# A hybrid recurrent and attention decoder trunk on one core: half of the first head pair's key transfers issued from ScalarE's queue

## The chip, the core and the metric

The kernel runs on one core of one Trainium2 chip. The metric is the device time of one execution in microseconds, the median over runs; lower is better. A core has five engines that work side by side, each through its own list of instructions in order: TensorE (PE, matrix products into the accumulator memory, PSUM), VectorE (DVE), ScalarE (ACT), GpSimd (POOL) and SyncE (SP, which here only issues transfers). They wait for each other through semaphores. Transfers (DMAs) are issued by an engine's queue and carried out by the core's 16 DMA engines.

## What is computed

A trunk of two layers over 1024 positions of width 1024: layer 0 mixes positions with a gated linear recurrence, layer 1 with stick-breaking attention of 16 heads of 64, and each is followed by a SwiGLU network of width 2816. The part around the change is the attention:

```
def stick_breaking_attention(x, w_qkv, w_o):
    qkv = jnp.einsum("bsd,de->bse", x, w_qkv).reshape(bsz, seq, 3, N_HEADS, HEAD_DIM)
    ...
    for blk in range(seq // Q_BLOCK):
        ...
        z = jnp.einsum("bhqd,bhkd->bhqk", qb, kb).astype(jnp.float32) * scale
        strict = s_idx < t_idx
        log_fail = jnp.where(strict, jax.nn.log_sigmoid(-z), 0.0)
        suffix = lax.cumsum(log_fail, axis=3, reverse=True) - log_fail
        weights = jnp.where(strict, jnp.exp(jax.nn.log_sigmoid(z) + suffix), 0.0)
        outs.append(jnp.einsum("bhqk,bhkd->bhqd", weights.astype(vb.dtype), vb))
    ...
    return jnp.einsum("bse,ed->bsd", o, w_o)
```

All of it is in float32. The kernel splits a float32 factor into a high part (a cast to a shorter format that PE multiplies fast) and a low part (the rest), and makes a product from three matmuls: high by high, high by low, low by high.

## The kernel before

**Stages.** The program goes through the recurrent layer, the first SwiGLU network, the attention, and the second SwiGLU network with the output projection. The first projection of the attention starts on PE at 941 us, the last at 1394 us.

**The attention's tiling.** Heads go in eight pairs q = 0 to 7; a pair fills the 128 partitions, head 0 of the pair (hx = 0) in the lower 64 and head 1 in the upper 64. For each pair there are three projections (`which` = 0 query, 1 key, 2 value), each in two halves of 512 positions (n = 0, 1), each in eight steps over the model width (tile `qk_ps`, lines 655 to 657, three matmuls a step). VectorE scales a finished half into `t` (line 2047), ScalarE casts it into the high part `qh` (line 2051), and VectorE subtracts to get the low part `ql` (line 2055). The names are the same for queries and keys.

**The transfers that the change is about.** Scores multiply over 128 partitions, in which a head's high and low query parts lie one above the other (tile `q`), while the head's key part is there twice: `kh` holds the high part in both halves of the partitions, `kl` the low part in both. So each half of a key (q, n) needs eight transfers of 64 partitions by 512 elements, from SBUF to SBUF: for head hx and y = 0 to 3, x = 4 hx + y; y // 2 picks `kh` or `kl`, and y % 2 the half of the partitions that is written. A query's half needs four. They are issued in `move`, line 2070, all from SyncE's queue. In the first pair there are 8 query and 16 key transfers.

**From scores to output.** A chunk of scores `z_ps` (line 2108) is two matmuls, `kh` by `q` and `kl` by `q`, for one block of 128 queries and 128 to 512 keys; two PSUM banks alternate, so a chunk is held back until ScalarE has taken the one before last. ScalarE's sigmoid turns it into `F` (line 2120), VectorE scans that along the keys (lines 2127, 2129), PE transposes the result into `wt_ps` (line 2139), ScalarE and VectorE split it into `th` and `tl`, and PE multiplies with the values (`av_ps`, line 2156). The first four chunks of a head take the first half of its keys, the fifth (query block 4, keys 3 and 4, 256 columns) spans both halves.

**What sets the order.** The order of instructions is made by a planner (`Plan`, lines 37 to 77), which knows each task's engine, an assumed duration, what it depends on and a rank. It starts, again and again, the task that can begin first, and by rank among equals; the order of starting is the order in every engine's list. The engine "dma" stands for SyncE's queue: an issue holds it 0.55 us and lands after the task's 2.4 us. `attention_plan` gives it the whole attention. The projections, of which the next pair's always wait to be done, are spread between the score chunks by their ranks. A task on an engine name that no other uses is a mere delay.

**Completion counters.** In the built program each transfer that SyncE or ScalarE issues counts up one of eight semaphores (DMAHW0 to DMAHW7), given out in turn in the order in which the planner issued them. Before a transfer is issued, its queue waits until the earlier one on the same counter has landed.

Of the kernel before, what the change touches and what calls it, by code (L numbers as in the profile page):

```python
# [245 lines left out]
def key_span(q, hx, j, ci):  # L246
    kbs = [kb for kb in range(j + 1) if key_spot(q, hx, j, kb)[0] == ci]
    return kbs[0] * P, len(kbs) * P


def attention_plan(plan, fn, at):
    NP, LEAD = HEADS // 2, 8
    diag = lambda h, js: [(*h, j, j // 4) for j in js]
# [19 lines left out]
    act = lambda n: 0.08 + n * 0.00082  # L273
# [4 lines left out]
    def weights(i, name, r, raw, use):  # L278
        ld = known.get(name) or plan.add("dma", 4.8, fn["load", name], [raw], r - 4)
        h0 = plan.add("act", 0.5, fn["whi", name, 0], [ld, use], r - 2.5)  # L280
        l0 = plan.add("dve", 0.6, fn["wlo", name, 0], [h0], r - 2.3)
        h1 = plan.add("act", 0.5, fn["whi", name, 1], [h0], r - 2.1)
        wlo[name] = (l0, plan.add("dve", 0.6, fn["wlo", name, 1], [h1, l0], r - 1.9))
        wraw[i] = wlo[name][1]
# [7 lines left out]
    for n in range(NH):  # L292
        t = plan.add("act", 0.5, fn["s_hi", n], [known["acc", n]], -17 + 2 * n)
        t = plan.add("dve", 1.2, fn["s_lo", n], [t], -17 + 2 * n)
        t = plan.add("pe", 0.46, fn["sums", n], [t], -17 + 2 * n)
        t = plan.add("act", 0.62, fn["root", n], [t], -17 + 2 * n, "root")
        t = plan.add("act", 0.5, fn["square", n], [t], -17 + 2 * n)
        t = plan.add("dve", 0.66, fn["newton", n], [t], -17 + 2 * n)
        factors.append(plan.add("dve", 0.66, fn["rbc", n], [t], -17 + 2 * n))
    for i, (q, which, n) in enumerate(groups):  # L300
        s, wi = 24 * (q - 1) + 4 * (i % 6), 3 * q + which
        if n == 0 and wi:
            weights(wi, (q, which), s, wraw.get(wi - 3), wuse.get(wi - 2))
        p = None
        for k in KS:
            need = [p]
            if p is None:
                need.append(pt.get(i - 4 if i in (4, 5) else i - 2) if i > 3 else None)
            if q == 0:
                need += [known.get(("x", k, n))]  # L310
            need.append(wlo[q, which][k // 4] if wi else known[q, which])
            p = plan.add("pe", 0.705, fn["proj", q, which, n, k], need, s + len(need) / 100 + KS.index(k) / 2 + 0.5)
        proj[i] = wuse[wi] = p
        s += 4
        turned_by = factors[n] if q == 0 else None
        if which < 2:
            order.append(i)
            was = order[-3] if len(order) > 2 else None
            pt[i] = plan.add("dve", 0.6, fn["t", q, which, n], [p, turned_by, *moves.get(was, ())], s + 0.1)
            th = plan.add("act", 0.5, fn["qh", q, which, n], [pt[i], *moves.get(was, ())], s + 0.2)  # L320
            tl = plan.add("dve", 0.6, fn["ql", q, which, n], [th], s + 0.3)
            old = [(zlast, q - 2)] if q > 1 else []
            for x in range(4 + 4 * which):
                src = (tl if x % 2 else th) if which == 0 else (tl if x // 2 % 2 else th)
                m = plan.add("dma", 2.4, fn["move", q, which, n, x], [src, *old], s + 0.3 + x / 100)
                moved.setdefault((q, which, n, x // (2 + 2 * which)), []).append(m)
                moves.setdefault(i, []).append(m)
        else:
            old = [(vadd, (q - 2, x)) for x in range(2)] if q > 1 else []
            pt[i] = plan.add("dve", 0.6, fn["t", q, which, n], [p, turned_by, *old], s + 0.1)  # L330
            before = (dv, (q, n - 1) if n else (q - 1, 1)) if q or n else None
            turned = (turn, (q, n - 1) if n else (q - 1, 1)) if q or n else None
            dv[q, n] = plan.add("dve", 0.66, fn["dv", q, n], [pt[i], before, turned], s + 0.4)
            if q == NP - 1:
                for y in range(NP - 1 - n):
                    back[y, n] = [
                        plan.add("dma", 2.4, fn["back", y, n, x], [p, (kept, (y, n))], s + 0.5 + y / 10) for x in range(2)
                    ]
# [3 lines left out]
    for c, (q, hx, j, ci) in enumerate(chunks):  # L342
        s, dg = c - LEAD, j // 4 == ci
        k0, n = key_span(q, hx, j, ci)
# [26 lines left out]
    for u, (q, hx, G, kb) in enumerate(units):  # L371
        if u in turns:
            v = turns[u]
            old = [(avlast, v[0] - 2)] if v[0] > 1 else []
# [5 lines left out]
        n = len(js) * P  # L380
# [10 lines left out]
        s = u + 1  # L391
# [15 lines left out]
    s, out = 24 * (NP - 1), []  # L407
# [112 lines left out]
def trunk(  # L520
# [15 lines left out]
    nc = tc.nc  # L536
    out_t = out[0 : D * LATE].rearrange("(d p c) -> d p c", p=P, c=LATE)
    out_r = out[D * LATE : D * S].rearrange("(r c) -> r c", c=D)
    f32 = lambda t: t.bitcast(F32)
# [321 lines left out]
    with ExitStack() as st:  # L861
# [153 lines left out]
        with tc.manual_schedule(engines={E.PE, E.Activation, E.DVE, E.Pool}):  # L1015
            plan = Plan(pe=28.5, dve=39.3, act=36.0, dma=20.0)
# [969 lines left out]
    with ExitStack() as st:  # L1986
# [15 lines left out]
        pair = lambda tag, q: [own([P, S], f"{tag}{2 * (q % 2) + hx}", F32R, tag) for hx in range(2)]  # L2002
        raws, W, PS, TT, TH, TL = {}, {}, {}, {}, {}, {}
        Q, KH, KL, VT, DV, VV, F_, Z = {}, {}, {}, {}, {}, {}, {}, {}
# [50 lines left out]
            V.tensor_sub(TL[n], TT[n], f32(TH[n]))  # L2055

        def move(q, which, n, x):
            if n == x == 0:
                if which == 0:
                    Q[q] = pair("q", q)  # L2060
                else:
                    KH[q], KL[q] = pair("kh", q), pair("kl", q)
            cs = slice(n * NB, (n + 1) * NB)
            hx, y = divmod(x, 2 + 2 * which)
            src = sides[hx]
            if which == 0:
                dst, t, to = Q[q][hx], (TH, TL)[y][n], sides[hx ^ y]
            else:
                dst, t, to = (KH, KL)[y // 2][q][hx], (TH, TL)[y // 2][n], sides[y % 2]
            nc.sync.dma_start(f32(dst)[to, cs], f32(t)[src])  # L2070

        def v_diff(q, n):
            DV[q, n] = own([P, NB], "dv")
# [112 lines left out]
        def ob_part(o, k):  # L2186
# [11 lines left out]
            "qh": q_hi,  # L2198
            "ql": q_lo,
            "move": move,  # L2200
            "dv": v_diff,
            "vt": v_turn,
# [41 lines left out]
        with tc.manual_schedule(engines={E.PE, E.Activation, E.DVE, E.Pool, E.SP}):  # L2244
            plan = Plan(pe=0.0, **pre["free"])
            chunks, units = attention_plan(plan, Steps(acts), pre["at"])
            plan.emit()
            mix.load(2)
# [60 lines left out]
```

## Time and profile before

| | before |
|---|---|
| runs | 2150.68, 2151.21, 2151.43 us |
| median | 2151.21 us |
| the profiled execution | 2151.21 us |
| its span, first to last instruction | 2149.4 us |
| mean granted clock of TensorE | 0.999 |
| busy in the span: PE | 2140.9 us |
| busy in the span: DVE, ACT | 1710.3 us, 1090.9 us |
| HBM read and written | 176.88 MB, 70.78 MB |

The span runs from the first instruction to the last; the execution's own time has 1.81 us more around it. Times in rows of a timeline are counted from the span's start. A row reads: start, duration, engine, source line, operation, output and inputs, and in brackets how long the engine was idle before it and what ended that. "SPq" and "ACTq" are issues of transfers by SyncE and ScalarE, which don't count as busy; "x2" means two in a row, whose duration is then that of both.

### The profile page before, as it was taken

The page shows a single profiled execution, that of the slowest core. Times are in us where ns is not written, and L with a number is a line of the kernel's source. Part 1 is how long each engine was busy: PE and PEld are TensorE (multiplying, and loading weights), DVE is VectorE, ACT ScalarE, POOL GpSimd, SP SyncE. Part 2 cuts the span into 40 slices and gives each one's busy share as a digit, 9 for nine tenths or more (in the row PEclk, how much of TensorE's full clock was granted, in tenths as well). Part 3 has the DMA queues.
Part 4 walks back from the last instruction along what each step waited for, and adds up shares of the span by engine and source line. Part 5 has one row for each costly group of instructions (what it writes and reads, how often), then busy time and mean ns, then how long its engine had stood idle before and what let it go on. Part 6 is the DMA issues. An engine that isn't in the chain of part 4 may idle for free.

```text
span 2149.4 us, 27088 instructions
## 1 busy us (share of the span) xinstructions
PE 2140.9 (100%) x9952; PEld 1784.5 (83%) x9952; DVE 1710.3 (80%) x2417; ACT 1090.9 (51%) x1795; POOL 29.3 (1%) x41
## 2 busy tenths in 40 slices
PE   9999999999999999999999999999999999999998
PEld 8888888888888888888888888888888888888887
DVE  8978679667777887888888888878877777788887
ACT  6677445344434544665555555544633444454555
POOL 0000020000000000000000000002000000000000
PEclk9999999999999999999999999999999999999999
DMA  4111312344454764444333333542234444467442
GB/s 178 40 49 50 128 40 88 99 137 147 133 162 133 274 203 126 147 143 104 98 98 96 101 99 97 175 148 80 73 104 128 152 134 150 146 233 240 137 155 86
DMA packets 133316, 274.61 MB, mean 128 GB/s; under 512 B 15296, under 2 KB 23872, under 8 KB 133184
## 3 DMA queue, kind: packets, MB, share of 16 engines
q1 hardware_dynamic: 132768, 272.36, 40.0%
q8 instruction: 78, 1.28, 0.2%
q10 hardware_dynamic: 416, 0.52, 0.1%
q14 instruction: 54, 0.44, 0.1%
HBM read 176.88 MB, written 70.78 MB: 115 GB/s over the span
## 4 chain that ended last, share of the span: by engine, by line
PE 99%; DVE 0%; DMA 0%; ACT 0%; issue 0%; SPq 0%; DVEq 0%
PE p_ps L1218 39%; PE p_ps L1222 19%; PE qk_ps L655 4%; PE qk_ps L657 4%; PE qk_ps L656 4%; PE av_ps L2156 3%; PE z_ps L2108 3%; PE wt_ps L2139 3%; PE ob_ps L657 2%; PE a_ps L655 2%; PE a_ps L656 2%; PE ob_ps L655 2%; PE a_ps L657 2%; PE ob_ps L656 2%; PE a_ps L809 1%; PE g_ps L656 1%
## 5 line engine op out<-in xcount | busy, mean ns | idle before, releaser
L1218 PE MATMUL p_ps<-vh,wch 128*128 128x512 f32 x524 | 203.9, 389 | 0.0
L1218 PE MATMUL p_ps<-vh,wbh 128*128 128x512 f32 x524 | 203.9, 389 | 0.0
L1218 PE MATMUL p_ps<-vl,wbh 128*128 128x512 f32 x524 | 203.9, 389 | 0.0
L1218 PE MATMUL p_ps<-vl,wch 128*128 128x512 f32 x524 | 203.9, 389 | 0.0
L1218 PE MATMUL p_ps<-vl,wah 128*128 128x512 f32 x524 | 203.8, 389 | 0.0
L1218 PE MATMUL p_ps<-vh,wah 128*128 128x512 f32 x524 | 203.8, 389 | 0.0
L1167 ACT CAST wbh<-sb 128x1024 fp32r<-128x1024 f32 (+2 forms) x69 | 69.6, 1009 | 188.6 <-DVE sb L1151 188.6
L2120 ACT ACTIVATE F<-z_ps 128x512 f32<-128x512 f32 (+3 forms) x188 | 88.6, 490 | 119.7 <-PE z_ps L2108 117.7
L1222 PE MATMUL p_ps<-vh,wbl 128*128 128x512 f32 x524 | 142.1, 389 | 0.0
L1222 PE MATMUL p_ps<-vh,wcl 128*128 128x512 f32 x524 | 141.8, 389 | 0.0
L1222 PE MATMUL p_ps<-vh,wal 128*128 128x512 f32 x524 | 141.8, 389 | 0.0
L2127 DVE TENSOR_TENSOR_SCAN F<-F,unit 128x256 f32<-128x256 f32 (+3 forms) x128 | 105.5, 845 | 38.4 <-ACT F L2120 38.1
L2144 ACT CAST th<-wt_ps 128x512 fp32r<-128x512 f32 x192 | 92.2, 480 | 64.3 <-PE wt_ps L2139 39.4
L1218 PEld LDWEIGHTS p_ps<-vh,wch 128*128 128x128 f32 x524 | 98.3, 188 | 20.6
L1218 PEld LDWEIGHTS p_ps<-vh,wbh 128*128 128x128 f32 x524 | 98.3, 188 | 20.6
L1222 PEld LDWEIGHTS p_ps<-vh,wcl 128*128 128x128 f32 x524 | 98.3, 188 | 20.5
L1222 PEld LDWEIGHTS p_ps<-vh,wbl 128*128 128x128 f32 x524 | 98.3, 188 | 20.5
L1222 PEld LDWEIGHTS p_ps<-vh,wal 128*128 128x128 f32 x524 | 98.3, 188 | 20.4
L1218 PEld LDWEIGHTS p_ps<-vh,wah 128*128 128x128 f32 x524 | 98.3, 188 | 20.4
L1218 PEld LDWEIGHTS p_ps<-vl,wah 128*128 128x128 f32 x524 | 98.3, 188 | 20.4
L1218 PEld LDWEIGHTS p_ps<-vl,wbh 128*128 128x128 f32 x524 | 98.4, 188 | 20.4
L1218 PEld LDWEIGHTS p_ps<-vl,wch 128*128 128x128 f32 x524 | 98.3, 188 | 20.4
(447 smaller groups left out, 5416.8 us busy)
## 6 DMA issues: line engine op xcount, KB each, us to landing
raw<-in_ffn_w_in SPq DMA_DIRECT2D x88, 512.0 KB, 3.7
vl<-pd SPq DMA_DIRECT2D x128, 256.0 KB, 3.6
pd<-U SPq DMA_DIRECT2D x90, 256.0 KB, 2.3
raw<-in_ffn_w_out SPq DMA_DIRECT2D x28, 512.0 KB, 4.0
raw<-in_attn_w_qkv SPq DMA_DIRECT2D x24, 512.0 KB, 3.6
kh<-qh SPq DMA_DIRECT2D x64, 128.0 KB, 2.3
kl<-ql SPq DMA_DIRECT2D x64, 128.0 KB, 2.3
acc<-pd SPq DMA_DIRECT2D x28, 256.0 KB, 2.6
```

The source lines that it names most:

```text
L655: nc.tensor.matmul(ps, lhsT=wh, rhs=mh, start=first, stop=False, **kw)
L656: nc.tensor.matmul(ps, lhsT=wh, rhs=ml, start=False, stop=False, **kw)
L657: nc.tensor.matmul(ps, lhsT=wl, rhs=mh, start=False, stop=last, **kw)
L1167: nc.scalar.copy(self.full(self.wb), self.full(self.sb))
L1218: nc.tensor.matmul(ps, lhsT=c(hi, j), rhs=t, start=j == x == 0 and not onto, stop=False, skip_group_check=onto)
L1222: nc.tensor.matmul(ps, lhsT=c(lo, j), rhs=rhs[j][0], start=False, stop=j == len(rhs) - 1, skip_group_check=onto)
L2108: nc.tensor.matmul(ps[:, 0:n], lhsT=lhsT, rhs=rhs, start=i == 0, stop=i == 1)
L2120: nc.scalar.activation(F, Z.pop(c)[:, 0:n], AF.Sigmoid, scale=-SC)
L2127: V.tensor_tensor_scan(rev, rev, unit[:, NB - n :][:, ::-1], 0.0, op0=ALU.mult, op1=ALU.add)
L2139: nc.tensor.transpose(tp[:, c : c + P], F_[q, hx, j, ci][:, k0 : k0 + P], ident)
L2144: nc.scalar.copy(WH[u][:, c:], TP[u][:, c:])
L2156: nc.tensor.matmul(ps[:, c:], lhsT=VV[q][:, kb, hx], rhs=t.pop(u)[:, c:], start=kb == 4 * G and i == 0, stop=kb == 3 and i == 1,)
```

## The change

Of the first head pair's key transfers (q = 0, which = 1), those with odd x, the ones that write the upper 64 partitions, are issued from ScalarE's queue; the other 8 key transfers, and all transfers of queries and of the other pairs, stay on SyncE's. For the planner such a transfer is a task of 0.6 us on ScalarE, ranked right behind the high cast, and a delay of 1.85 us till it lands. Since the two kinds can now be started in either order, the tiles `q`, `kh` and `kl` of a pair are taken at the pair's first transfer, whichever it is.

```
+by_act = lambda q, which, x: q == 0 and which == 1 and x % 2
 ...
             for x in range(4 + 4 * which):
                 src = (tl if x % 2 else th) if which == 0 else (tl if x // 2 % 2 else th)
-                m = plan.add("dma", 2.4, fn["move", q, which, n, x], [src, *old], s + 0.3 + x / 100)
+                if by_act(q, which, x):
+                    m = plan.add("act", 0.6, fn["move", q, which, n, x], [src], s + 0.25)
+                    m = plan.add(("landing", which, n, x), 1.85, fn["wait", 0], [m])
+                else:
+                    m = plan.add("dma", 2.4, fn["move", q, which, n, x], [src, *old], s + 0.3 + x / 100)
 ...
         def move(q, which, n, x):
-            if n == x == 0:
-                if which == 0:
-                    Q[q] = pair("q", q)
-                else:
-                    KH[q], KL[q] = pair("kh", q), pair("kl", q)
+            if which == 0 and q not in Q:
+                Q[q] = pair("q", q)
+            if which == 1 and q not in KH:
+                KH[q], KL[q] = pair("kh", q), pair("kl", q)
 ...
-            nc.sync.dma_start(f32(dst)[to, cs], f32(t)[src])
+            (nc.scalar if by_act(q, which, x) else nc.sync).dma_start(f32(dst)[to, cs], f32(t)[src])
```

No matmul, cast, scan or transfer is added or left out. The planner's order changes on PE, VectorE and ScalarE around the first score chunks (between about 963 and 991 us of the profile before); the lists ahead of that stretch and behind it are the same.

## Prediction

> **What bounds the kernel now.** I read the page's first part, then the waits of TensorE (PE).
>
> ```profile
> span 2149.4 us, 27088 instructions
> PE 2140.9 (100%) x9952; PEld 1784.5 (83%) x9952; DVE 1710.3 (80%) x2417; ACT 1090.9 (51%) x1795; POOL 29.3 (1%) x41
> ```
>
> ```profile
> PE a_ps L795 <- DVE rbc L581: 1.1, 1, 1.1
> PE z_ps L2108 <- DMA kl<-ql: 0.3, 1, 0.3
> ```
>
> PE works through 2140.9 of 2149.4 us, and the waits view (us in total, times, longest) knows one wait of it after the start: for a key transfer. So any new wait of PE is added in full, and the change, which removes no work of PE, can gain hardly more than that one wait. The timeline of PE shows it (start, duration, operation, idle time before it):
>
> ```profile
> 969.40 0.22 PE L2108 MATMUL z_ps<-kh,q 128*128 128x128 f32 x1
> 969.86 0.40 PE L655 MATMUL qk_ps<-xg,whi 128*128 128x512 f32 x1
> 970.55 0.33 PE L2108 MATMUL z_ps<-kh,q 128*128 128x384 f32 x1
> 970.90 0.40 PE L2108 MATMUL z_ps<-kh,q 128*128 128x512 f32 x1
> 971.36 0.40 PE L655 MATMUL qk_ps<-xg,whi 128*128 128x512 f32 x1
> 973.41 0.28 PE L2108 MATMUL z_ps<-kh,q 128*128 128x256 f32 x1
> 973.99 0.36 PE L2108 MATMUL z_ps<-kl,q 128*128 128x256 f32 x1 [0.30 <-DMA kl<-ql]
> 974.18 0.28 PE L2108 MATMUL z_ps<-kh,q 128*128 128x256 f32 x1
> 974.30 0.28 PE L2108 MATMUL z_ps<-kl,q 128*128 128x256 f32 x1
> ```
>
> An undisturbed pair of 256 columns starts 0.12 us apart (974.18, 974.30), the waiting pair 0.58: the wait costs 0.46 us (the page's 0.30 counts from the modelled end). Next, SyncE's queue and the landing of its transfers:
>
> ```profile
> 959.37 1.18 SPq L2070 DMA_DIRECT2D q<-qh  x2
> 963.20 1.19 SPq L2070 DMA_DIRECT2D q<-ql  x2
> 964.49 1.19 SPq L2070 DMA_DIRECT2D kh<-qh  x2
> 965.78 1.18 SPq L2070 DMA_DIRECT2D kl<-ql  x2
> 973.42 1.24 SPq L2070 DMA_DIRECT2D kl<-ql  x2
> 974.70 10.59 SPq L636 DMA_DIRECT2D raw<-in_attn_w_qkv  x2
> ```
>
> ```profile
> kh<-qh SPq DMA_DIRECT2D x8, 128.0 KB, 2.4
> kl<-ql SPq DMA_DIRECT2D x8, 128.0 KB, 2.3
> ```
>
> From 959.37 to 973.42 there are 22 issues, one in 0.64 us, and each lands about 2.3 us after its issue. Whether a second queue helps depends on the 16 DMA engines behind it. By stretch of time (in each row the last two numbers are the engines' busy share and GB/s):
>
> ```profile
> 15.00:20.00 5.00, 5.00 (x23) 4.14 (x23) 5.00 (x9) 5.00 (x10) 0.00 (x0) 1.00 1.06 393
> 965.00:970.00 5.00, 5.00 (x26) 4.22 (x25) 2.57 (x5) 2.21 (x4) 0.00 (x0) 1.00 0.89 206
> 970.00:975.00 5.00, 4.70 (x26) 3.85 (x25) 3.98 (x7) 2.12 (x6) 0.00 (x0) 1.00 0.89 204
> ```
>
> Loads at the kernel's start move 393 GB/s with full engines. The key transfers, between two halves of 64 partitions, keep them 0.89 busy at 206. In 5 us that is 1.03 MB, 7.9 transfers of 131 KB, in 4.45 busy us: 0.57 us of all engines for each. SyncE's queue leaves 0.07 us free between two.
>
> **The change part by part.** *PE's order.* The first scores of head 0, before and now (z_ps; qk_ps are projections; the line numbers now stand 6 or 7 higher):
>
> ```order
> L655 MATMUL qk_ps<-vh_3_2495,whi 128x512
> L656 MATMUL qk_ps<-vl_3_2496,whi 128x512
> L657 MATMUL qk_ps<-vh_3_2495,wlo 128x512
> L2108 MATMUL z_ps<-kh,q 128x128
> L2108 MATMUL z_ps<-kl,q 128x128
> L2108 MATMUL z_ps<-kh,q 128x256
> L2108 MATMUL z_ps<-kl,q 128x256
> L655 MATMUL qk_ps<-xg_6070,whi 128x512
> L656 MATMUL qk_ps<-xg_6071,whi 128x512
> L657 MATMUL qk_ps<-xg_6070,wlo 128x512
> L2108 MATMUL z_ps<-kh,q 128x384
> ```
>
> ```order
> L2114 MATMUL z_ps<-kh,q 128x128
> L2114 MATMUL z_ps<-kl,q 128x128
> L2114 MATMUL z_ps<-kh,q 128x256
> L2114 MATMUL z_ps<-kl,q 128x256
> L662 MATMUL qk_ps<-vh_3_2495,whi 128x512
> L663 MATMUL qk_ps<-vl_3_2496,whi 128x512
> L664 MATMUL qk_ps<-vh_3_2495,wlo 128x512
> L2114 MATMUL z_ps<-kh,q 128x384
> L2114 MATMUL z_ps<-kl,q 128x384
> L662 MATMUL qk_ps<-xg_6070,whi 128x512
> L663 MATMUL qk_ps<-xg_6071,whi 128x512
> L664 MATMUL qk_ps<-xg_6070,wlo 128x512
> ```
>
> The planner believes the keys come sooner, and puts one projection step of three matmuls (0.69 us: 970.55 - 969.86) behind the first two score chunks. PE now asks for the first keys at 968.71, and has fewer projections left with which to fill a wait.
>
> *ScalarE's order.* From its cast of the first key half on (x2: two in a row), before and now:
>
> ```order
> L2021 CAST whi<-raw 128x512 x2
> L2051 CAST qh_7712<-t_7705 128x512
> L2120 ACT_TABLE_LOAD
> L2120 ACTIVATE F_7743<-z_ps 128x128
> L2120 ACTIVATE F_7749<-z_ps 128x256
> L2120 ACTIVATE F_7761<-z_ps 128x384
> ```
>
> ```order
> L2076 DMA kh<-qh_7683 64x512 x2
> L2076 DMA kl<-ql_7693 64x512 x2
> L2058 CAST qh_7713<-t_7701 128x512
> L2076 DMA kh<-qh_7713 64x512 x2
> L2076 DMA kl<-ql_7719 64x512
> L2126 ACT_TABLE_LOAD
> L2126 ACTIVATE F_7736<-z_ps 128x128
> L2076 DMA kl<-ql_7719 64x512
> L2126 ACTIVATE F_7746<-z_ps 128x256
> L2028 CAST whi<-raw 128x512
> L2126 ACTIVATE F_7759<-z_ps 128x384
> L2028 CAST whi<-raw 128x512
> ```
>
> Seven issues now stand ahead of the sigmoid table's load and one behind the first sigmoid; two half weight casts went in between the sigmoids. PE has two banks for scores, so chunk c+2 waits for sigmoid c. Their times before, and the nearest rows for an issue:
>
> ```profile
> 963.23 0.62 ACT L2051 CAST qh<-t 128x512 fp32r<-128x512 f32 x1 [1.40 <-DVE t L2047]
> 963.94 1.14 ACT L2021 CAST whi<-raw 128x512 fp32r<-128x512 f32 x2
> 965.96 0.62 ACT L2051 CAST qh<-t 128x512 fp32r<-128x512 f32 x1 [0.89 <-DVE t L2047]
> 966.60 1.28 ACT L2120 ACT_TABLE_LOAD   x1
> 969.77 0.67 ACT L2120 ACTIVATE F<-z_ps 128x128 f32<-128x128 f32 x2 [1.89 <-PE z_ps L2108]
> 971.10 1.06 ACT L2120 ACTIVATE F<-z_ps 128x384 f32<-128x384 f32 x2 [0.65 <-PE z_ps L2108]
> 0.75 0.41 ACTq L768 DMA_DIRECT2D xr<-in_x  x1
> ```
>
> ```profile
> L2070 SPq DMA_DIRECT2D kl<-ql x64: 540/595/1031, 965.8 to 1381.7; - x64
> ```
>
> ScalarE's one issue in this trace took 0.41 us; the same transfers on SyncE's queue took 0.54 to 1.03, median 0.60. I take 0.60, the same transfer's row, and keep 0.41 and 1.03 as ends. Then: cast ends 963.85, four issues to 966.25, second cast to 966.9, three issues (the first waits for the cast) to 968.75, table load to 970.05, first sigmoid (0.34) to 970.4. Before, table load and sigmoid were done by 967.9 and 970.1, and hidden.
>
> *The queues' coupling.* SyncE's key transfers, before and now (7693 and 7685 are head 0's first parts; a DMAHW is one of eight completion counters that all transfers take in turn):
>
> ```order
> L2070 DMA kh_7693<-qh0_7683 64x512 [waits DMAHW7_49,Activation_49]
> L2070 DMA kh_7693<-qh0_7683 64x512 [waits DMAHW0_49]
> L2070 DMA kl_7695<-ql0_7691 64x512 [waits DMAHW1_49,DVE_49]
> L2070 DMA kl_7695<-ql0_7691 64x512 [waits DMAHW2_49]
> L2070 DMA kh_7694<-qh0_7683 64x512 [waits DMAHW3_49]
> ```
>
> ```order
> L2076 DMA kh_7685<-qh0_7683 64x512 [waits DMAHW2_49,Activation_49]
> L2076 DMA kh_7686<-qh0_7683 64x512 [waits DMAHW4_49]
> L2076 DMA kl_7687<-ql0_7693 64x512 [waits DMAHW5_49,DVE_49]
> L2076 DMA kl_7688<-ql0_7693 64x512 [waits DMAHW7_49]
> L2076 DMA kh_7685<-qh1_7713 64x512 [waits DMAHW1_49,Activation_49]
> L2076 DMA kh_7686<-qh1_7713 64x512 [waits DMAHW3_49]
> ```
>
> Two things moved. Head 1's parts (7686, 7688) now come between head 0's, which PE needs first. And a transfer waits until the one eight places earlier has landed; that was always an old one of the same queue, but now DMAHW5 is that of ScalarE's first key transfer, issued only at 963.85.
>
> *The sum.* Between 963.2 and 966.3 the two queues issue eight transfers, 4.6 us of engine time in 3.1 us: a backlog of 1.5 us grows. (a) ScalarE's first transfer lands at 966.2, or 966.8 with one queued ahead; SyncE then issues head 0's low part, which lands 2.3 us later at 969.1, with 0.8 of remaining backlog at 969.9, where PE has asked at 968.8: +1.0 to 1.1, taken 1.0 (0 without backlog: 966.2 + 2.3 = 968.5). (b) The first sigmoid now follows its scores at about 970.6; PE reaches chunk 2 at about 971.0, so no wait. Behind it ScalarE's last issue waits for the counter of its own transfer of 966.95, which with backlog lands near 971: 0.4 later than the sigmoid's end, and chunk 3 waits for its sigmoid 0.4. Chunk 4 waits for the sigmoid of chunk 2, behind 0.6 issue, 0.38, half cast 0.57, 0.53 = 2.1 us, while PE has only 0.35 + 0.69 + 0.46 = 1.5 us of work: 0.5. (c) Chunk 4 needs head 0's second half. Before, all 24 transfers ended at 976.35 (last issue 974.06 + 2.3) and head 0's at 973.85. Filled engines can save 24 x 0.07 = 1.7 us in all, so the end is near 974.7 and head 0's last part, now among the last, near 974.4; PE comes to it at about 973.4: +1.0. Together 1.0 + 0.4 + 0.5 + 1.0 = 2.9, less the 0.46 that goes: +2.4 us.
>
> The Trainium skill speaks against the change here: "SBUF — State Buffer", section "Can I just issue two DMAs to hit both halves?", says that two transfers at once, one on each half of the partitions, moved only 6% more than one. This trace agrees as far as it goes (0.89 busy at half the load's rate), but has no two queues at once.
>
> *What I cost at nothing.* The low halves of the value weights move on VectorE behind the first scans:
>
> ```profile
> 964.59 0.69 DVE L2025 TENSOR_TENSOR wlo<-raw,whi 128x512 fp32r<-128x512 f32 x1
> 974.80 1.27 DVE L2127 TENSOR_TENSOR_SCAN F<-F,unit 128x256 f32<-128x256 f32 x2 [1.02 <-ACT F L2120]
> 980.34 0.47 PE L655 MATMUL qk_ps<-xg,whi 128*128 128x512 f32 x1
> ```
>
> PE first uses them at 980.34, later by the new waits. They now stand behind the scan of chunk 5, whose scores come at about 975.2 and whose sigmoid at 976: two scans of 256 (0.63 each) and two subtractions (0.61 apart) end near 978.5. That cover of 2 us hides them; were they 3 us late, 1 us would show. The next weight load (974.70) moves back by some 4 us with the casts that free its buffer, and its rows are wanted a head pair later.
>
> **The rivals.** *Only ScalarE's queue counts* (the two queues' transfers, which go to different halves, do not slow each other; for it: the loads' 393 GB/s shows that the engines can do twice 206). Landing stays 2.3 us, (a) and (c) vanish, PE reaches chunk 2 at 968.71 + 0.46 + 0.69 = 969.86 and waits for the first sigmoid until 970.45: 0.6; chunk 4 0.5; chunk 5, by the same chain, 0.2. 1.3 - 0.46 = +0.8: 2152.0 us. *The gain comes*: issues take 0.41 us, seven of them free 1.3 us, and nothing waits but some 0.1 us: -0.4, 2150.8 us. *ScalarE's issues are dear*, the one on the other side: at 1.05 us each (just above the longest kl row), seven put the table load 3.15 us later, first sigmoid to 973.55; chunk 2 waits 3.7, chunk 3 0.45, chunks 4 and 5 0.7: 4.85 - 0.46 = +4.4, 2155.6 us. It decides from 1.04 us on, where it passes 0.2% (4.3 us, about what a measurement of this kernel can tell from no change); that half of the 64 kl rows take 0.595 or less, on the other queue, speaks against it.
>
> **How the numbers follow.** The profiled execution took 2151.21 us, which is the median of the runs, its span 2149.4, so the sum is laid on 2151.21. Chances: forecast (shared engines) 0.50, 2153.6 us; ScalarE alone 0.26; gain 0.12; dear issues 0.12, of which nearly all lie above 0.2%. No case reaches a gain of 4.3 us, since the only wait is 0.46; 0.02 for what I have not seen. So faster 0.02, same 0.87, slower 0.11. The range goes from the gain's end, 2150.7, to past the dear issues, 2156.2.
>
> **What would show it.** Right: PE waiting at line 2114 for kl at the first chunk and at the fifth, each near 1 us; landing of the key transfers grown from 2.3 to 3 us or more; busy share near 1 with GB/s hardly over 220. If landing stays 2.3 and GB/s rises towards 300, the second case holds, with waits of z_ps for F. ScalarE's issue rows tell 0.41, 0.60 or 1. Wrong altogether: PE's idle time outside 968 to 980 us, or another order on the chip than planned.

## The result and the profile after

| | before | after |
|---|---|---|
| median | 2150.77 us (21 runs, 2150.54 to 2151.43) | 2154.37 us (21 runs, 2153.49 to 2155.08) |
| ratio, 95% interval | | 1.0016 (1.0010 to 1.0022) |
| profiled execution, its span | 2151.21, 2149.4 us | 2154.52, 2152.7 us |
| PE busy in the span | 2140.9 us | 2141.4 us |

The change costs 3.6 us, just inside the 0.2% that the prediction took for no difference. PE does the same work, so the time must stand in its waits. The waits of PE in the profile after (us in total, times, longest):

```profile
PE a_ps L802 <- DVE rbc L588: 1.1, 1, 1.1
PE z_ps L2114 <- DMA kl<-ql: 3.0, 2, 2.3
```

The wait at the program's start is as before. The one for keys was 0.3 us, once, and is now 3.0 us, twice. PE's timeline shows where:

```profile
968.99 0.22 PE L2114 MATMUL z_ps<-kh,q 128*128 128x128 f32 x1
971.53 0.30 PE L2114 MATMUL z_ps<-kl,q 128*128 128x128 f32 x1 [2.33 <-DMA kl<-ql]
971.67 0.33 PE L2114 MATMUL z_ps<-kh,q 128*128 128x256 f32 x1
...
973.69 0.39 PE L2114 MATMUL z_ps<-kh,q 128*128 128x512 f32 x1
973.92 0.39 PE L2114 MATMUL z_ps<-kl,q 128*128 128x512 f32 x1
974.39 0.35 PE L2114 MATMUL z_ps<-kh,q 128*128 128x256 f32 x1
975.39 0.36 PE L2114 MATMUL z_ps<-kl,q 128*128 128x256 f32 x1 [0.64 <-DMA kl<-ql]
```

By starts, as the prediction counted: the first pair of matmuls is 2.54 us apart instead of 0.06 (in the queue_alone kernel below it isn't held), so the first chunk waits 2.48 us for head 0's low part. The fifth starts 0.24 us late (974.39 - 973.92 - 0.23) and waits 0.88 us between its two matmuls (1.00 - 0.12): 1.12. The late start is a wait for the second half's high part, which landed at 974.30; the other wait is for its low part. None of the chunks waits for a sigmoid. 2.48 + 1.12 - 0.46 (the old wait) = 3.1 us.

What the first chunk waits for is seen in the two queues. SyncE's issues, then ScalarE's instructions:

```profile
963.49 1.19 SPq L2076 DMA_DIRECT2D q<-ql  x2
964.77 1.19 SPq L2076 DMA_DIRECT2D kh<-qh  x2
967.08 1.71 SPq L2076 DMA_DIRECT2D kl<-ql  x2
970.44 1.10 SPq L2076 DMA_DIRECT2D kh<-qh  x2
```

```profile
964.16 1.42 ACTq L2076 DMA_DIRECT2D kh<-qh  x2
965.68 1.74 ACTq L2076 DMA_DIRECT2D kl<-ql  x2
967.52 0.62 ACT L2058 CAST qh<-t 128x512 fp32r<-128x512 f32 x1 [3.39 <-DMA kh<-qh]
...
969.97 1.28 ACT L2126 ACT_TABLE_LOAD   x1 [1.83 <-issue]
```

SyncE is free at 965.96 and the low part exists (ScalarE issues its copy of it at 965.68), yet SyncE's `kl` is issued at 967.08. In the trace's records of single transfers ScalarE's first key transfer landed at 967.02: SyncE stood 1.12 us on the completion counter that it shares with that transfer. Then this `kl` took 4.32 us to land, at 971.40, and PE went on at 971.53.

SyncE stood so a second time, ahead of the transfers that the fifth chunk waits for. It was free again at 968.79, and the second half's high part existed (ScalarE issues its copy of it at 968.17), yet SyncE's `kh` is issued at 970.44, 0.07 us after ScalarE's first `kl` had landed (970.37). These 1.65 us are longer than the fifth chunk's whole wait of 1.12.

The median landing of the first pair's key transfers:

```profile
kh<-qh ACTq DMA_DIRECT2D x4, 128.0 KB, 3.7
kh<-qh SPq DMA_DIRECT2D x4, 128.0 KB, 3.7
kl<-ql ACTq DMA_DIRECT2D x4, 128.0 KB, 4.4
kl<-ql SPq DMA_DIRECT2D x4, 128.0 KB, 3.9
```

Before it was 2.4 and 2.3. The DMA engines' share and GB/s, the last two numbers of a stretch of time:

```profile
965.00:970.00 5.00, 4.21 (x20) 3.29 (x18) 1.15 (x2) 0.65 (x2) 0.00 (x0) 1.00 0.95 248
970.00:975.00 5.00, 3.13 (x14) 2.30 (x14) 2.58 (x5) 3.92 (x7) 0.00 (x0) 1.00 0.86 212
```

In these rows two queues move at most 248 GB/s where one moved 206: a transfer takes 1.5 to 1.9 times as long to land, for a fifth more throughput. That is what the Trainium skill says in "DMA: Bandwidth & Descriptors", section "Issuing engines are not separate DMA queues": transfers of all issuers end on the same 16 DMA engines and interleave. The rows agree with it. They agree with what the prediction cited from the Trainium skill on two halves too, except that the gain was a fifth and not 6%.

### The profile page after: what moved, and what is told of

Read it like the earlier page. It is cut to its first block, busy times and chain, and to the rows that moved or that the text cites. A ratio compares the mean times of both kernels' runs of the same rounds, so it can differ in the third digit from the quotient of the medians.

```text
span 2152.7 us, 27088 instructions
## 1 busy us (share of the span) xinstructions
PE 2141.4 (99%) x9952; PEld 1784.9 (83%) x9952; DVE 1710.2 (79%) x2417; ACT 1092.2 (51%) x1795; POOL 29.3 (1%) x41
## 3 DMA queue, kind: packets, MB, share of 16 engines
q8 instruction: 78, 1.28, 0.2%
## 4 chain that ended last, share of the span: by engine, by line
PE 99%; DMA 0%; DVE 0%; ACT 0%; ACTq 0%; SPq 0%; issue 0%; DVEq 0%
PE p_ps L1225 38%; PE p_ps L1229 19%; PE qk_ps L662 4%; PE qk_ps L664 4%; PE qk_ps L663 4%; PE av_ps L2162 3%; PE z_ps L2114 3%; PE wt_ps L2145 3%; PE a_ps L664 2%; PE ob_ps L663 2%; PE ob_ps L664 2%; PE a_ps L663 2%; PE a_ps L662 2%; PE ob_ps L662 2%; PE a_ps L816 1%; PE g_ps L664 1%
```

## Experiments

Each kernel has 11 runs beside 21 or 33 of the kernel before on the same chip (the change itself has 21). The same kernel, run again, came out by 0.03 and 0.35 us otherwise, so a second measure stands beside them: the time from the start of PE's 4,001st matmul to that of its 5,400th from the end. These are the same two matmuls in every kernel (at 908.89 and 1023.30 us before, 114.41 us apart), and the stretch between holds everything that any of the kernels reorders. It is read from one execution of each kernel; between the two pairs of repeats it differs by 0.14 and 0.03 us. All rows of the table are against before, in us; the waits are those that the profile shows on PE in this stretch.

| kernel | median | ratio, 95% interval | the stretch | PE's waits in it |
|---|---|---|---|---|
| the change | +3.6 | 1.0016 (1.0010 to 1.0022) | +3.12 | key 2.33, key 0.64 |
| order_alone | +2.0 | 1.0009 (1.0001 to 1.0018) | +2.19 | key 0.64, 0.42, 0.99 |
| queue_alone | -0.6 | 0.9998 (0.9989 to 1.0007) | -0.53 | none |
| small_act | +0.7 | 1.0004 (0.9995 to 1.0013) | +0.70 | key 0.40, sigmoid 0.18 |
| head0_first | +0.7 | 1.0004 (0.9995 to 1.0013) | +0.90 | sigmoid 0.49, key 0.22 |
| priced | +1.6 | 1.0007 (0.9998 to 1.0016) | +2.03 | sigmoid 0.73, key 0.98 |
| both | +0.2 | 1.0000 (0.9992 to 1.0009) | +1.23 | sigmoid 1.51 |
| table_early | +0.7 | 1.0003 (0.9994 to 1.0012) | +0.17 | sigmoid 0.31 |
| by_head | +4.0 | 1.0018 (1.0009 to 1.0028) | +5.16 | key 2.77 |
| by_head_priced | +2.2 | 1.0009 (1.0000 to 1.0018) | +1.88 | key 1.33, 0.40 |
| queue_again | -0.6 | 0.9997 (0.9988 to 1.0006) | -0.39 | none |
| queue_all | -0.9 | 0.9996 (0.9988 to 1.0005) | -0.54 | none |
| queue_all_again | -0.5 | 0.9999 (0.9990 to 1.0007) | -0.51 | none |

**Theories of the first four runs.** A: the loss needs both, the planner's new order of PE's work, made for keys that land early, and the second queue's data on DMA engines that the two queues share. B: the second queue with its issues brings it by itself, whatever it carries. C: the new order brings it by itself.

### The order without the queue, and the queue without the order

order_alone keeps the changed plan but issues all 16 key transfers from SyncE, in the order of before:

```
+        calls = defaultdict(int)
         def move(q, which, n, x):
+            if q == 0 and which == 1:
+                x = calls[n]
+                calls[n] += 1
...
-            (nc.scalar if by_act(q, which, x) else nc.sync).dma_start(f32(dst)[to, cs], f32(t)[src])
+            nc.sync.dma_start(f32(dst)[to, cs], f32(t)[src])
```

> Planner's new order on every engine, but all 16 key transfers issued by SyncE in the old order (head 0's four first). Theory A (two queues share the DMA engines): every landing is back at 2.3 us; the first chunk waits 0 to 0.3 us, but PE now asks for head 0's second key half at about 971.5 instead of 973.5 while it still lands near 973.9, so the fifth chunk waits about 2.4 us: +2.0 us against the kernel before, so more than half of the change's +3.6 is the order's. Rival B (ScalarE's issuing time delays the sigmoids): no issue is on ScalarE, so the time is back at the kernel before, within 0.5 us. Rival C (the order alone): +3.6 us, as the change.

queue_alone keeps the plan of the kernel before and only takes the other queue:

```
-            nc.sync.dma_start(f32(dst)[to, cs], f32(t)[src])
+            by_act = q == 0 and which == 1 and x % 2
+            (nc.scalar if by_act else nc.sync).dma_start(f32(dst)[to, cs], f32(t)[src])
```

> Planner's old order, but the key transfers with odd x are issued from ScalarE's queue where the old order has them. Theory A: landings grow to 3 or 4 us, but PE asks later (969.4 and 973.5) and head 0 keeps its place ahead of head 1, so the waits are small: -0.4 to +0.8 us. Rival B: eight issues of 0.6 to 1.0 us on ScalarE, five of them ahead of the table load, cost what they cost in the change: +2 to +3.6 us. Rival C: no change of order, no cost: within 0.3 us of the kernel before.

The order alone costs 2.0 us, as A had it, but not quite by A's waits: by starts the first chunk waits 0.80 us (A had at most 0.3) and the fifth 1.81 (A had 2.4). PE's timeline of order_alone has three waits where before had one:

```profile
969.72 0.30 PE L2119 MATMUL z_ps<-kl,q 128*128 128x128 f32 x1 [0.64 <-DMA kl<-ql]
...
972.93 0.35 PE L2119 MATMUL z_ps<-kh,q 128*128 128x256 f32 x1 [0.42 <-DMA kh<-qh]
974.27 0.35 PE L2119 MATMUL z_ps<-kl,q 128*128 128x256 f32 x1 [0.99 <-DMA kl<-ql]
```

The queue alone costs nothing. The waits view of queue_alone has no key in it, although its transfers land as slowly as in the change:

```profile
PE a_ps L795 <- DVE rbc L581: 1.1, 1, 1.1
```

```profile
kh<-qh ACTq DMA_DIRECT2D x4, 128.0 KB, 3.7
kh<-qh SPq DMA_DIRECT2D x4, 128.0 KB, 3.8
kl<-ql ACTq DMA_DIRECT2D x4, 128.0 KB, 4.0
kl<-ql SPq DMA_DIRECT2D x4, 128.0 KB, 3.8
```

So B falls, with the same eight issues on ScalarE: here a landing of 4 us harms nothing. The old plan issues head 0's four parts first from both queues, and PE asks at 968.80 us for keys of which the last landed at 968.17; it has 9 more projection matmuls ahead of the fifth chunk than the change. Even the old wait of 0.46 us is gone, a little more than A's -0.4. C falls too: the order alone is +2.0, not the whole.

Since +2.0 and -0.6 don't add up to +3.6, the order and the two queues together lose another 2.2 us, or 1.5 by the stretch (3.12 - 2.19 + 0.53).

### What the two lose together

small_act is the change with ScalarE's transfers cut from 512 columns to 8; the rest of those copies is cleared by GpSimd, so that most of the upper halves of the keys is left out of the scores. Order, counters and number of issues stay.

```
+            if by_act(q, which, x):
+                c0 = n * NB
+                nc.scalar.dma_start(f32(dst)[to, c0 : c0 + 8], f32(t)[src, 0:8])
+            else:
+                nc.sync.dma_start(f32(dst)[to, cs], f32(t)[src])
```

> The change, but each of ScalarE's eight transfers moves 8 columns instead of 512 (the rest of the keys' upper copies is left at zero, cleared beforehand by GpSimd): same orders, same number of issues, the DMA engines get half the data. Theory A: SyncE's landings are back at 2.3 us, the first chunk waits under 0.4, the fifth under 0.5, what is left is ScalarE's issuing time before the sigmoids: 0 to +1.2 us. Rival B: the issues are all still there: +3 to +3.6 us. Rival C: +3 to +3.6 us.

head0_first holds head 1's parts back, in the plan, until the low part is there, so both queues issue head 0's four parts first:

```
-                src = (tl if x % 2 else th) if which == 0 else (tl if x // 2 % 2 else th)
+                src = (tl if x % 2 else th) if which == 0 else (tl if x // 2 % 2 or q == 0 and x > 3 else th)
```

> The change, but for the planner head 1's key parts wait for the low part too, so that both queues issue head 0's parts ahead of head 1's; SyncE's first kl then no longer waits for a counter of a ScalarE transfer. Theory A: same load on the engines (landings 3 to 4.5 us), but head 0's first low parts are issued 1.5 us sooner: the first chunk waits 0 to 0.5 instead of 2.5 us, the fifth up to 1.5: +0.5 to +1.8 us. Rival B: as many issues on ScalarE: +3 to +3.6 us. Rival C: the order of PE around the first chunks is nearly the change's: +3 us.

Both fell to +0.7 us. In small_act SyncE's transfers land in 2.4 us again, and the first wait for a key is 0.40 us instead of 2.33 (PE's timeline):

```profile
968.57 0.30 PE L2118 MATMUL z_ps<-kl,q 128*128 128x128 f32 x1 [0.40 <-DMA kl<-ql]
```

SyncE still stood on a shared counter here: after its `kh` pair it was free at 964.89 us and issued `kl` at 966.25, 0.07 us after one of ScalarE's had landed. So that coupling by itself costs little as long as transfers land in 2.4 us, and without the second queue's data on the DMA engines most of the change's first wait goes. In the change both delay the same low part: SyncE issued it 1.12 us later than it could, and it took 4.32 us. In head0_first the engines are as full as in the change (its landings are 3.7 and 3.8 us), but both halves of head 0 are issued ahead of head 1's: the first chunk is held 0.28 us by its starts, too short for the profile to list, and the fifth 0.22 us. What shows in their place, as the largest wait, is the first sigmoid, for which the third chunk waits:

```profile
PE z_ps L2114 <- ACT F L2126: 0.5, 1, 0.5
...
PE z_ps L2114 <- DMA kl<-ql: 0.2, 1, 0.2
```

head0_first takes away the counter's wait before head 0's low part and the mixing of the heads at once; how the two share its gain wasn't tried. PE's order isn't quite the change's either: three more projection matmuls (0.7 us) stand ahead of the fourth and fifth chunk, so part of what the fifth gained is theirs.

### Telling the planner the true landing

From here on the theories are sharper. A: PE's order was made for transfers that land in 2 us, and on the shared engines they take nearly 4. B: two queues lose it through the longer landing, wherever the chunks stand (for the split by heads: transfers of different halves don't slow each other). C: ScalarE's issues hold up the table load and the sigmoids behind them.

priced is the change with 3.9 us for a landing, in place of 1.85 and 2.4:

```
-                    m = plan.add(("landing", which, n, x), 1.85, fn["wait", 0], [m])
+                    m = plan.add(("landing", which, n, x), 3.9, fn["wait", 0], [m])
                 else:
-                    m = plan.add("dma", 2.4, fn["move", q, which, n, x], [src, *old], s + 0.3 + x / 100)
+                    m = plan.add("dma", 3.9 if q == 0 and which else 2.4, fn["move", q, which, n, x], [src, *old], s + 0.3 + x / 100)
```

> The change, but the planner is told what the landing of the first pair's key transfers took on the chip when two queues were at work: 3.9 us instead of 1.85 (ScalarE's) and 2.4 (SyncE's). It then puts the first score chunk 9 matmuls (three projection steps, 2.1 us) further back than the change has it, and the fifth chunk 9 as well. Theory A (the loss is an order of PE made for transfers that land in 2 us, on DMA engines that both queues share and that take nearly 4): PE asks at 971.1 instead of 969.0, the first low part is there at 971.4, at most 0.5 us of waits for keys is left, and the time is -0.6 to +0.6 us against before. Theory B (the two queues as such lose it, through the longer landing, wherever the chunks stand): +2 to +3.6 us. Theory C (ScalarE's issues hold up its table load and sigmoids): the waits for keys go and waits for sigmoids of the same size come, +1.5 to +3.6 us.

A expected too much of this: it took away a third (by the stretch) to half (by the median) of the loss. By its median the kernel lies in C's range, and below B's. The first chunk hardly waits for keys any more (0.28 us by its starts); in the profile PE now waits for the first sigmoid and for the fifth chunk's key:

```profile
972.83 0.44 PE L2114 MATMUL z_ps<-kh,q 128*128 128x384 f32 x1 [0.73 <-ACT F L2126]
...
975.70 0.36 PE L2114 MATMUL z_ps<-kl,q 128*128 128x256 f32 x1 [0.98 <-DMA kl<-ql]
```

The new price leaves the counters as they were, and the planner doesn't know them: after its `kl` pair SyncE was free at 968.42 us, and issued the second half's first `kh` at 969.81, 0.06 us after a transfer of ScalarE's on the same counter had landed.

The kernel named both joins this with head0_first.

> The two mends together: the planner is told 3.9 us for the landing of the first pair's key transfers, and head 1's parts are held back until the low part is there, so that both queues issue head 0's four parts first. Measured apart they gave +1.6 us (the price alone) and +0.7 us (head 0 first alone). Theory A (two causes, PE's order and the order of the heads, and no third): no wait of PE for a key over 0.3 us, as with the queue alone in the order of before, and -0.6 to +0.4 us against before. Theory C (with the key waits gone, ScalarE's eight issues ahead of its table load come to the fore, as the 0.73 us wait for a sigmoid with the price alone suggests): PE waits 0.4 to 1.0 us for the first sigmoid, +0.4 to +1.2 us.

No wait for a key is left, as A had it, but 1.51 us for the first sigmoid, more than C had it. ScalarE's timeline shows why: all eight issues stand ahead of the table load, the last two alone from 969.17 to 971.33 us.

```profile
969.17 0.81 ACTq L2076 DMA_DIRECT2D kh<-qh  x1
970.01 1.32 ACTq L2076 DMA_DIRECT2D kl<-ql  x1
971.36 1.28 ACT L2126 ACT_TABLE_LOAD   x1 [2.50 <-DMA kl<-ql]
972.66 0.55 ACT L2126 ACTIVATE F<-z_ps 128x128 f32<-128x128 f32 x2
```

In queue_alone five issues stand ahead of it, and it begins at 967.92. So C had a part: a third cause was hidden behind the key waits. Its median, +0.2, is lower than its stretch of +1.23 makes likely; the expectation can't be decided by the median, only by the wait.

table_early puts the table load ahead of the issues:

```
             nc.scalar.copy(TH[n], TT[n])
+            if q == which == 0 and n == 1:
+                nc.scalar.activation(own([P, 1], "early"), f32(TH[n])[:, 0:1], AF.Sigmoid)
```

> The two mends together, and besides a sigmoid of one column on ScalarE behind the last query cast, whose result nothing uses: with it ScalarE's table load comes ahead of its eight issues instead of behind them (there it started at 971.36 us, and PE waited 1.51 us for the first sigmoid). Theory (that wait is the table load's 1.28 us, pushed back by the issues): PE's wait for the sigmoid falls to 0.1 to 0.4 us, and the time to -0.9 to -0.1 us against before, -1.2 to -0.7 against the two mends alone. Rival (the issues themselves hold the sigmoid, since the last of them ends at 971.3 us whatever the table): the wait stays above 1.0 us and the time within 0.3 us of the two mends alone.

The wait went from 1.51 to 0.31 us, by nearly the table load's 1.28:

```profile
961.37 1.28 ACT L2060 ACT_TABLE_LOAD   x1
...
971.58 0.55 ACT L2128 ACTIVATE F<-z_ps 128x128 f32<-128x128 f32 x2 [2.78 <-DMA kl<-ql]
```

So the rival falls, and the stretch is +0.17 us. The expectation missed the time as a whole, though, which isn't better than both's: +0.7 us, where -0.9 to -0.1 was expected. Behind the stretch, PE's matmuls lose about 0.1 us in each following head pair (0.7 us to the end), with no wait in the profile and the same list of instructions. Where that comes from stays open.

### Another split, and the granted clock

by_head gives ScalarE head 1's transfers (sources in the upper 64 partitions) and SyncE head 0's.

```
-by_act = lambda q, which, x: q == 0 and which == 1 and x % 2
+by_act = lambda q, which, x: q == 0 and which == 1 and x > 3
```

> The change with another split: ScalarE issues all of head 1's key transfers (sources in the upper 64 partitions), SyncE all of head 0's (sources in the lower 64). Theory A (both queues draw on the same 16 DMA engines, whichever partitions they read): key transfers still land 3.4 to 4 us after their issue while both queues are at work, GB/s in 965 to 970 us is 240 to 260, and as head 0 now has only one queue, PE waits 0.5 to 2 us for it: +0.5 to +2.0 us against before. Theory B (transfers that read different halves of the partitions don't slow each other): landing 2.3 to 2.6 us, GB/s towards 400, no wait for keys of over 0.3 us, -0.6 to +0.3 us. Theory C (ScalarE's issues): +2 to +3.6 us, as eight issues stand on it here too.

by_head_priced is that with 3.9 us for a landing.

> The split by heads with the landing priced at 3.9 us, so that PE asks for its first key some 1.5 to 2 us later than it did with the split by heads, where it waited 2.77 us and its granted clock was 0.65 in 970 to 980 us. Theory A (the clock fell because PE stood still that long, and the rest of that kernel's +4.0 us was waits as in the change): first wait 0.4 to 1.4 us, clock 1.00 in 970 to 980 us, +1.0 to +2.2 us against before. Rival (the clock falls whenever ScalarE issues this set of transfers, by their load): clock 0.7 or less again and +3 us or more. Landing stays 3.8 to 4.6 us in both.

Transfers that read different halves share the engines as well: by_head's landings are no shorter.

```profile
kh<-qh SPq DMA_DIRECT2D x4, 128.0 KB, 4.1
...
kl<-ql SPq DMA_DIRECT2D x4, 128.0 KB, 3.8
```

But +4.0 us was more than A had, whose range ended at +2.0. One part is a longer wait, one the clock. PE's timeline, and PE by stretches of 1 us (first number after the comma PE's busy time; third from the right the granted clock):

```profile
969.25 0.22 PE L2114 MATMUL z_ps<-kh,q 128*128 128x128 f32 x1
972.24 0.45 PE L2114 MATMUL z_ps<-kl,q 128*128 128x128 f32 x1 [2.77 <-DMA kl<-ql]
```

```profile
970.00:971.00 1.00, 0.00 (x0) 0.00 (x0) 0.83 (x2) 0.92 (x2) 0.00 (x0) 1.00 1.08 236
971.00:972.00 1.00, 0.00 (x0) 0.00 (x0) 0.00 (x0) 0.98 (x1) 0.00 (x0) 0.77 1.04 240
972.00:973.00 1.00, 0.76 (x3) 0.79 (x4) 0.00 (x0) 0.28 (x1) 0.00 (x0) 0.50 1.08 246
...
978.00:979.00 1.00, 1.00 (x5) 0.82 (x5) 0.85 (x2) 0.50 (x2) 0.00 (x0) 0.82 0.00 0
```

While PE stood, its clock fell to 0.50 (at 971.54 us by the trace's clock records) and came back at 978.37. The first wait is 2.93 us by starts (2.99 - 0.06), less the old 0.46: 2.5 of the stretch's 5.16 us. The likely rest is the clock: PE worked again from 972.24 on, so 6.1 us of work ran at half clock, which by estimate can cost up to 3.1 us. With the longer landing in the plan, PE's wait was shorter and the clock stayed at 1.00, as A had it:

```profile
971.50 0.30 PE L2114 MATMUL z_ps<-kl,q 128*128 128x128 f32 x1 [1.33 <-DMA kl<-ql]
```

```profile
970.00:975.00 5.00, 3.30 (x16) 2.30 (x14) 3.83 (x7) 3.54 (x7) 0.00 (x0) 1.00 1.01 249
```

### Is the queue alone faster than before?

queue_again is the same kernel as queue_alone; queue_all gives ScalarE every second key transfer of all eight pairs, in the plan of before, and queue_all_again repeats that.

```
-            by_act = q == 0 and which == 1 and x % 2
+            by_act = which == 1 and x % 2
```

> The queue alone in the order of the kernel before, once more, because its first ratio (0.9998, 0.9989 to 1.0007) didn't resolve 0.6 us. Theory A (PE's only wait for keys, 0.46 us, is gone, and nothing takes its place): -0.8 to -0.2 us against before, no wait of PE for a key. Rival (the first result was noise between runs): -0.2 to +0.3 us.

> The queue alone, in the order of the kernel before, and for the key transfers of all eight head pairs: 64 transfers on ScalarE instead of 8. Theory A (only a wait of PE can be gained; PE waits for no key of the later pairs, and ScalarE has the time): the same as with the first pair alone, -1.0 to +0.3 us against before. Theory C (issues on ScalarE, which took 0.47 to 1.04 us beside SyncE's, hold up the sigmoids and casts that stand behind them in the later pairs, when ScalarE has work between every two score chunks): each pair loses up to 0.5 us, +1 to +4 us.

> The queue alone for the key transfers of all eight pairs in the order of the kernel before, once more: the first result was 0.9996, 0.9988 to 1.0005, -0.9 us. Theory (the one wait for a key is gone, nothing is added): -1.0 to -0.3 us against before again. Rival (noise between runs): -0.3 to +0.3 us.

Four out of four lie 0.5 to 0.9 us below before, each interval still reaches past 1, and the profiles of all four have no wait for a key and a stretch shorter by 0.39 to 0.54 us: the old wait of 0.46. They beat both kernels, by 0.03% against before, which only the repeats and the trace carry. 56 more issues on ScalarE neither gain nor cost anything that can be seen; the one key wait of before was in the first pair.

## Why the prediction was right in its direction and short in size

- **Bound, and what can be gained.** Right: PE's busy time stayed, every new wait came in full, and the most that any version gained in the stretch, 0.54 us, is about the old wait of 0.46.
- **(a), the first chunk.** The mechanism was right step by step: ScalarE's first transfer landed at 967.02 (forecast 966.2 to 966.8), SyncE's `kl` was issued 0.06 us later. The term was mis-sized: landing was taken as 2.3 plus 0.8 us of backlog, and took 4.32. So 2.48 us instead of 1.0. The backlog was worked out as if it only shrank from there; but both queues went on issuing while this transfer was on its way, and the engines were 0.95 busy between 965 and 970 us, so it probably shared them all the time. The throughput was forecast as hardly over 220 GB/s, and was 248.
- **(b), two waits for sigmoids, 0.9 us.** Not in the change: the first chunk held PE for 1.5 us longer than forecast, and ScalarE had caught up by then. So they weren't added to (a). With (a) gone, or nearly, another sigmoid shows in their place: head0_first (0.49), priced (0.73) and both (1.51) wait for the first one, at the third chunk, where the prediction's main case had no wait (its first rival had 0.6 there).
- **(c), the fifth chunk, 1.0 us.** 1.12, but the size is right in part by luck. PE was ready for it at 974.15, not 973.4, and head 0's last part landed at 975.25, not 974.4; 0.26 us of each is the later start of the whole stretch, and the rest of the two errors cancels. The forecast put the landing down to filled engines alone; SyncE's second stand on a counter, 1.65 us, was not in it.
- **The sum.** 2.9 - 0.46 was forecast, 3.6 - 0.46 = 3.1 is in the trace and +3.12 in the stretch. The two profiled executions differ by 3.3 us: 0.26 more stands ahead of the stretch, where the kernels are the same, and 0.08 less behind it. The medians say 3.6. Some of the nearness is luck: 1.5 too little in (a) and 0.9 too much in (b) partly cancel, and the forecast time of 2153.6 us was laid on the median of three runs, 0.44 us above that of 21.
- **Costed at nothing.** Right, with more to spare than the 2 us of the forecast: the value weights' low halves were ready at 979.05, and PE's first matmul with them, in the next projection, started at 984.17.

```profile
977.78 1.27 DVE L2032 TENSOR_TENSOR wlo<-raw,whi 128x512 fp32r<-128x512 f32 x2
984.17 0.40 PE L664 MATMUL qk_ps<-xg,wlo 128*128 128x512 f32 x1
```

- **Issues of 0.60 us.** The first seven took 0.54, 0.86, 0.67, 1.04, 0.47, 0.61 and 0.55, mean 0.68. They were dear in part, but well below the 1.05 of the rival, and in the change hidden by the key waits.
- **The rivals.** That only ScalarE's queue counts fell with the landings. The gain came only without the new plan. That the plan by itself costs 2 us on one queue was in none of the cases: the prediction saw PE ask earlier, and counted it only in the two waits.

## What to carry to other kernels

A transfer's landing time in a planner is not a constant of the transfer: when a second queue runs on the same engines, put in what it takes with both at work, or keep an order that asks late enough. Here the first alone took away a third to half of the loss, and the second all of it. Look at the order in which transfers reach the shared engines before adding issuers, and at completion counters that tie the queues together. When a wait goes, the next one may be what it was covering, here a table load behind the issues of the same engine.

## What the runs showed of the hardware

- An issue on ScalarE's queue took 0.41 us alone in the trace before (another transfer, `xr`), and 0.47 to 1.42 us for the first pair's keys while SyncE issued as well (1.42 in the kernel named both); SyncE's took up to 1.05 in queue_alone (the same 16 transfers before: 0.54 to 0.60).
- Two queues of transfers between 64-partition halves moved 235 (queue_all_again) to 261 GB/s (priced) between 965 and 970 us, against 206 from one. Most landed 3 to 5 us after their issue, against 2.3.
- The granted clock fell to 0.50 in by_head 2.07 us after PE had stopped (at 971.54; the last matmul had ended at 969.47), and stayed there for 6.83 us, though PE worked again after 0.70 of them. The 2.33 us for which PE stood still in the change left it at 1.00. The length alone didn't decide: behind the kernel's last matmul the clock fell after 1.90 us in by_head, and only after 5.27 us in the change. The trace's stretches of one clock are whole multiples of 3.413 us (in by_head 965.97, 6.83 and 1170.77 us, which are 283, 2 and 343 of them; in the change 2143.57, which is 628), so in these runs the clock changed only on a fixed grid, and where a standstill fell on the grid counted. The Trainium skill, "TensorE: Matmul & The Clock Gate", Part 1, gives an idle window of about 3.4 us that runs freely. The runs agree with the free running, but here about 2 us of standing still before a step of the grid was enough.
